# A state space mixer inside an fp32 trunk: two weight units split a layer early, Pool's operations cut, norms in one bank, the last steps in a written order

## The chip, the cores and the metric

One core of a Trainium2 chip runs the whole program. The metric is the device time of one execution in microseconds (us). The engines are TensorE (PE; PEld is its weight load, which overlaps the matmuls), VectorE (DVE), ScalarE (ACT), GpSimd (POOL) and SyncE (SP), which here only issues transfers. Each engine works through its own list of instructions in order, so an instruction that waits holds up all that stands behind it on that engine.

## What is computed

A trunk of two layers on 256 tokens of width 1024, all in float32. Each layer adds half of a SwiGLU network, then a mixer, then half of a second SwiGLU network. The first layer's mixer is the state space one (Mamba-2), which the change touches; the second's is latent attention.

```python
for i in range(2):
    x = x + 0.5 * swiglu(rms_norm(x, ...), ...)
    h = rms_norm(x, norm_w[i, 1])
    x = x + (mamba2_mixer(h, ...) if i == 0 else mla_mixer(h, ...))
    x = x + 0.5 * swiglu(rms_norm(x, ...), ...)

def mamba2_mixer(h, ...):
    proj = h @ w_in                          # z 2048, x 2048, B 1024, C 1024, dt 32
    xbc = silu(causal_depthwise_conv(xbc))   # 4 taps over time
    y = ssd_chunked(xs, softplus(dt + dt_bias), a, bm, cm) + d_skip * xs
    g = y * silu(z)                          # 8 groups of 256 channels
    g = g * rsqrt(mean(g * g over the group) + EPS)
    return (g * norm_w) @ w_out
```

## The kernel before

**Weights.** All weights arrive as one stream of units, mostly of eight 128x128 tiles (512 KB, one transfer on SP's queue). Each unit is split in two reduced parts, a high one by a cast on ACT (`whi`, L131) and the remainder by a subtraction on DVE (`wlo`, L134). A product of a weight tile with an activation is then three matmuls of 256 columns (`mm3`, L227 to L229: high with high, high with low, low with high). There are four raw buffers (AHEAD) and five split ones (SPLIT), so the cast of a unit waits until TensorE has finished with the unit five places ahead of it.

**The mixer.** `ssm` works on eight groups g of 256 channels. It first computes dt, and B and C for the groups 0 and 1, and then runs a loop over g, whose body is written as a list of stages:

- `stage_x` and `stage_z`: two projections each of eight tiles; x goes through `conv` (DVE L421, ACT L431 and L435, one POOL addition of 128x512 in L436, four DVE operations in L439, a Silu on ACT in L443).
- `stage_y(g-1)`: eight small matmuls with the decay matrices `dec` (L609, L612), then on DVE `y` (L619), on POOL the gating `gt` of 128x512 (L624) and the squares of both halves and their sum (`gsq`, L263, L266, L267).
- `stage_a` for two groups on every other turn: decay matrices, by sixteen exponentials on ACT (L569, L572) and masks and products on DVE.
- `stage_bc(g+2)`: B and C of a later group.
- `stage_n(g-1)`: the column sums of the squares on TensorE (L273), then `rsv` on DVE (L277) and a power on POOL that gives `rsc` (L281).
- `stage_t(g)`: x transposed on TensorE (L590), and `xd` on DVE (L595).
- `stage_o(g-2)`, written ahead of `stage_z`: `rsc` spread over the partitions by TensorE (L288), the normalised `gn` on DVE (L639), and its two parts `yh` on ACT (L252) and `yl` on DVE (L253).
- `stage_out(g-3)`: sixteen tiles of the output weights with `yh` and `yl`, 48 matmuls, added up over the groups in the four PSUM banks called acc. The projections use acc banks until the first `stage_out` and after that the four misc banks, as all small results do.

Behind the loop a list of stages finishes the groups 5 to 7. Text names below such as n2 or o7 are `stage_n(2)` or `stage_o(7)`, and y7 likewise.

**Order.** The code's order is only a priority. A scheduler simulates all engines and puts the instructions of each in the order in which they come ready, so that matmuls of several stages interleave.

Of the kernel before, what the change touches and what calls it, by code (L numbers as in the profile page):

```python
# [10 lines left out]
F32 = mybir.dt.float32  # L11
F32R = mybir.dt.float32r
# [7 lines left out]
P = 128  # L20
T = 256
# [44 lines left out]
EARLY = (MLA0 + 6, MLA0 + 11, MLA0 + 12, MLA0 + 17)  # L66


class Stream:
# [15 lines left out]
    def load(self, upto):  # L85
        while self.loaded < min(upto, len(self.sizes)):
            u = self.loaded
            if u in EARLY:
# [17 lines left out]
    def cut(self, upto):  # L106
        while self.split < min(upto, len(self.sizes)):
            u = self.split
            if u in EARLY:
                self.split += 1  # L110
                continue
# [34 lines left out]

    def early(self, pool, u):
# [6 lines left out]
        hi = pool.tile([P, n], F32R, tag=f"hi{u}", name=f"hi{u}", bufs=1)  # L154
        lo = pool.tile([P, n], F32R, tag=f"lo{u}", name=f"lo{u}", bufs=1)
        self.nc.scalar.copy(hi, raw[:, :n])
        self.nc.gpsimd.tensor_tensor(
            out=lo, in0=raw[:, :n], in1=hi.bitcast(F32), op=ALU.subtract
        )
        self.parts[u] = (hi, lo)  # L160
# [25 lines left out]
def trunk(ctx: ExitStack, tc: tile.TileContext, xt, pos, wts, small, consts, out):  # L186
# [81 lines left out]

    def rs_col(acc, n):

        ps = misc_ps()
        for b in range(NB):
# [3 lines left out]
        v = sp.tile([P, NB], F32, tag="rsv", name="rsv")  # L276
        nc.vector.tensor_scalar(  # L277
            out=v, in0=ps[:, :NB], scalar1=1.0 / n, scalar2=EPS, op0=ALU.mult, op1=ALU.add
        )
# [4 lines left out]
    def spread(r):  # L284

        ps = misc_ps()
        for b in range(NB):
# [116 lines left out]

    def ssm(n, nxt):
        with tc.tile_pool(name="mp", bufs=2) as mp:
# [10 lines left out]
            def conv(ps, tiles, dst):  # L417
# [12 lines left out]
                for j, t in enumerate(tiles):  # L430
# [4 lines left out]
                    nc.scalar.activation(b[:, j], up[:, j, 1 : 1 + T], AF.Copy, scale=w(t, 1))  # L435
                nc.gpsimd.tensor_tensor(out=a, in0=a, in1=b, op=ALU.add)  # L436
                for k in (2, 3):
# [103 lines left out]
            def stage_a(g):  # L541
# [10 lines left out]
                nc.scalar.copy(cb, ps[:, : 3 * P])  # L552
                acb = mp.tile([P, 4, T], F32, tag="acb", name="acb")
                nc.sync.dma_start(
# [10 lines left out]
                for hp in range(2):  # L565
                    dec = mp.tile([P, 2, 3 * P], F32, tag="dec", name="dec", bufs=6)
                    for j in range(2):
# [35 lines left out]
            def stage_y(g):  # L603
# [19 lines left out]
                gt = mp.tile([P, 2, T], F32, tag="gt", name="gt")  # L623
                nc.gpsimd.tensor_tensor(out=gt, in0=y, in1=zs, op=ALU.mult)  # L624
                sq = sp.tile([P, T], F32, tag="xsq", name="gsq")
                for j in range(2):
                    add_square(sq, gt[:, j], j == 0)
                st[g, "g"], st[g, "q"] = gt, sq

            def stage_n(g):  # L630
                st[g, "r"] = rs_col(st.pop((g, "q")), 2 * P)

            def stage_o(g):
                gt = st.pop((g, "g"))
                ps = spread(st.pop((g, "r")))
                gn = mp.tile([P, 2, T], F32, tag="tmp", name="gn", bufs=3)
# [41 lines left out]
            def stage_z(g):  # L678
# [7 lines left out]
                st[g, "z"] = zs  # L686

            stage_bc(1)
            last = NG - 1
            for g in range(NG):  # L690
                stage_x(g)
                if g == 0:
                    bias, acd = sums()
                if g > 1:
                    stage_o(g - 2)
                stage_z(g)
# [5 lines left out]
                if g + 2 < NG:  # L702
                    stage_bc(g + 2)
                if g:
                    stage_n(g - 1)
                if g < last:
                    stage_t(g)
                if g > 2:
                    stage_out(g - 3)

            stage_t(last)
            stage_o(last - 1)
            stage_out(last - 2, 0, 4)
# [417 lines left out]
    for i, (f, n) in enumerate(plan):  # L1131
        nxt = n + 1 if i + 1 < len(plan) else None
        if i == 3:
            ep = early.enter_context(tc.tile_pool(name="ep", bufs=1))
# [157 lines left out]
```

## Time and profile before

| | us |
|---|---|
| three runs | 1102.43, 1103.98, 1105.25 |
| median of them | 1103.98 |
| the profiled execution | 1104.49 |
| its span, first to last instruction | 1102.7 |
| TensorE busy in it | 1079.8 |
| the mixer's part of the span | 195.0 to 428.7 |

The profile is of one execution. Its time is 1104.49 us, of which the span covers 1102.7. Busy times overlap between engines. An idle time of TensorE stands in brackets in its row, with the instruction that it waited for. The granted clock stands as a share of full speed: 1.00 is 2.4 GHz and 0.50 is 1.2 GHz.

### The profile page before, as it was taken

The numbers are of one execution on the slowest core, as the hardware profiler recorded it, in microseconds if no ns is written. First come the engines' busy times: TensorE is split into PE (matmuls) and PEld (weight loads), VectorE is DVE, ScalarE is ACT, GpSimd is POOL, SyncE is SP. The second block draws the span as 40 slices with busy tenths as digits, with TensorE's granted clock in tenths as the row PEclk, the third lists the DMA queues.
The fourth block names the chain that finished last, engine by engine and source line by source line (L and its number), as shares of the span: only waits on it lengthen the run. The fifth ranks groups of instructions, "written<-read, shape, count | busy, mean of one in ns | idle before, by whom it ended". The sixth has DMA issues, their size and how long they took to land.

```text
span 1102.7 us, 18308 instructions
## 1 busy us (share of the span) xinstructions
PE 1079.8 (98%) x6886; PEld 964.3 (87%) x6886; DVE 838.8 (76%) x1396; ACT 643.1 (58%) x1105; POOL 195.7 (18%) x201
## 2 busy tenths in 40 slices
PE   8999999999899998999999999999999999999998
PEld 7888888998899998888888988888898688888887
DVE  7877766789978867877777688876779868877663
ACT  6755644667876744666544476664458546655541
POOL 1100013213523235000012101001240544000000
PEclk9999999999999998999999999999999999999999
DMA  8656655565445453655555566655531325656661
GB/s 287 213 189 190 184 188 170 173 197 190 161 163 178 135 185 97 208 187 184 184 191 189 174 210 211 212 196 187 175 105 59 97 87 167 214 186 188 191 200 49
DMA packets 55640, 191.58 MB, mean 174 GB/s; under 512 B 6240, under 2 KB 9088, under 8 KB 55552
## 3 DMA queue, kind: packets, MB, share of 16 engines
q1 hardware_dynamic: 55488, 190.41, 53.0%
q8 instruction: 54, 0.88, 0.3%
q14 instruction: 34, 0.28, 0.1%
q0 software_dynamic: 64, 0.01, 0.0%
HBM read 189.31 MB, written 1.08 MB: 173 GB/s over the span
## 4 chain that ended last, share of the span: by engine, by line
PE 61%; DVE 2%; ACT 0%; issue 0%; ACTq 0%; DVEq 0%
PE acc L238 32%; PE misc L238 17%; PE acc L227 2%; PE acc L228 2%; PE acc L229 2%; PE acc L1072 1%; PE acc L248 1%; PE acc L247 1%; PE acc L249 1%; PE misc L963 1%; PE misc L1032 1%; PE misc L1057 0%; DVE pr L1050 0%; DVE mx L1041 0%; PE misc L1033 0%; PE misc L273 0%
## 5 line engine op out<-in xcount | busy, mean ns | idle before, releaser
L134 DVE TENSOR_TENSOR wlo<-raw,whi 128x1024 fp32r<-128x1024 f32 (+2 forms) x345 | 429.4, 1247 | 155.0 <-ACT whi L131 153.8
L131 ACT CAST whi<-raw 128x1024 fp32r<-128x1024 f32 (+2 forms) x353 | 362.8, 1032 | 252.5 <-PE acc L238 132.9
L238 PE MATMUL misc<-xp,whi 128*128 128x512 f32 x704 | 277.9, 398 | 0.5 <-DVE xp L257 0.5
L238 PE MATMUL acc<-xp,whi 128*128 128x512 f32 x704 | 275.5, 395 | 0.0
L238 PE MATMUL acc<-ap,whi 128*128 128x512 f32 x616 | 215.5, 397 | 0.0
L238 PE MATMUL acc<-xp,wlo 128*128 128x256 f32 x704 | 196.8, 281 | 0.0
L238 PE MATMUL misc<-xp,wlo 128*128 128x256 f32 x704 | 196.4, 281 | 0.3 <-DVE wlo L134 0.2
L238 PE MATMUL acc<-ap,wlo 128*128 128x256 f32 x616 | 167.8, 281 | 0.0
L238 PEld LDWEIGHTS acc<-xp,whi 128*128 128x128 f32 x704 | 131.9, 188 | 32.2
L238 PEld LDWEIGHTS misc<-xp,whi 128*128 128x128 f32 x704 | 131.9, 188 | 24.2 <-DVE xp L257 0.8
L238 PEld LDWEIGHTS misc<-xp,wlo 128*128 128x128 f32 x704 | 132.5, 188 | 8.2 <-DVE wlo L134 0.9
L238 PEld LDWEIGHTS acc<-ap,whi 128*128 128x128 f32 x616 | 113.9, 188 | 25.5
L238 PEld LDWEIGHTS acc<-xp,wlo 128*128 128x128 f32 x704 | 132.8, 189 | 0.7
L238 PEld LDWEIGHTS acc<-ap,wlo 128*128 128x128 f32 x616 | 115.4, 188 | 2.8
L346 ACT COPY g<-misc 128x256 f32<-128x256 f32 x88 | 32.7, 371 | 77.1 <-PE misc L238 77.1
L228 PE MATMUL acc<-xp,whi 128*128 128x256 f32 x264 | 74.6, 283 | 0.0
L227 PE MATMUL acc<-xp,whi 128*128 128x256 f32 x264 | 74.5, 283 | 0.0
L229 PE MATMUL acc<-xp,wlo 128*128 128x256 f32 x264 | 74.2, 281 | 0.0
L263 POOL TENSOR_TENSOR xsq<-x 128x256 f32<-128x256 f32 x5 | 3.1, 612 | 284.8 <-DVE x L402 271.4
L266 POOL TENSOR_TENSOR sq<-x 128x256 f32<-128x256 f32 x35 | 31.7, 912 | 111.2 <-DVE x L402 111.2
L347 DVE TENSOR_TENSOR g<-misc,g 128x256 f32<-128x256 f32 x88 | 37.0, 420 | 18.0 <-ACT g L346 18.0
L227 PEld LDWEIGHTS acc<-xp,whi 128*128 128x128 f32 x264 | 49.7, 189 | 0.3 <-issue 0.3
(260 smaller groups left out, 1889.5 us busy)
## 6 DMA issues: line engine op xcount, KB each, us to landing
raw<-wts SPq DMA_DIRECT2D x341, 512.0 KB, 3.7
acb<-acd SPq DMA_DIRECT2D x8, 512.0 KB, 3.8
raw<-wts SPq DMA_DIRECT2D x8, 256.0 KB, 4.9
raw<-wts SPq DMA_DIRECT2D x4, 384.0 KB, 3.2
x<-xt SPq DMA_DIRECT2D x8, 128.0 KB, 4.5
out<-x SPq DMA_DIRECT2D x8, 128.0 KB, 3.5
raw<-wts SPq DMA_DIRECT2D x4, 192.0 KB, 2.4
sm<-small SPq DMA_DIRECT2D x1, 283.5 KB, 6.4
```

The costliest lines, as they stand in the source:

```text
L131: self.nc.scalar.copy(hi[:, c], raw[:, c])
L134: ins = eng.tensor_tensor(out=lo[:, c], in0=raw[:, c], in1=hi[:, c].bitcast(F32), op=ALU.subtract)
L227: nc.tensor.matmul(o, w[0], h, start=start, stop=False)
L228: nc.tensor.matmul(o, w[0], l, start=False, stop=False)
L229: nc.tensor.matmul(o, w[1], h, start=False, stop=stop)
L238: nc.tensor.matmul(dst, a, b, start=start and i == 0, stop=stop and i == 1)
L247: nc.tensor.matmul(o, h, w[0], start=start, stop=False)
L248: nc.tensor.matmul(o, l, w[0], start=False, stop=False)
L249: nc.tensor.matmul(o, h, w[1], start=False, stop=stop)
L266: nc.gpsimd.tensor_tensor(out=sq, in0=src, in1=src, op=ALU.mult)
L346: nc.scalar.copy(t, ps[:, T:])
L347: nc.vector.tensor_tensor(out=t, in0=ps[:, :T], in1=t, op=ALU.add)
```

## The change

Five edits, all to the mixer but for the first, which reaches into the network ahead of it.

1. The four units of B and C of the groups 0 and 1 (`EARLY_BC`) are loaded and split during the first network, at its steps q = 4, 8, 12 and 16, the high part on ACT and the rest on DVE. They lie in a new pool `sep`, in the buffers that later hold `dec` and `acb`.
2. POOL's operations: the convolution's addition and the gating are each two operations of 128x256 in place of one of 128x512. The squares are one operation on ACT (128x512, L643 of the new code) and one addition on POOL (128x256, L644), in place of three on POOL.
3. `rsv` in `stage_n` is computed by ACT (L288 of the new code) and no more by DVE.
4. `stage_o(g-2)` and `stage_n(g-1)` share one misc bank and stand together behind `stage_bc` (`stage_on`), so that o of a group is now one turn behind its n, at the end of the turn.
5. The stages behind the loop, with the last `stage_out` of the loop, stand in TensorE's list as written (`manual_schedule`): y7 and n6 come sooner, and n and o of the last groups lie between parts of `stage_out`.

```diff
+EARLY_BC = tuple(SSM0 + n for n in range(1, 5))
...
         self.nc.scalar.copy(hi, raw[:, :n])
-        self.nc.gpsimd.tensor_tensor(
+        eng = self.nc.gpsimd if tags is None else self.nc.vector
+        eng.tensor_tensor(
             out=lo, in0=raw[:, :n], in1=hi.bitcast(F32), op=ALU.subtract
         )
...
+        if by_act:
+            nc.scalar.activation(v, ps[:, :NB], AF.Copy, scale=1.0 / n, bias=EPS)
+        else:
+            nc.vector.tensor_scalar(
+                out=v, in0=ps[:, :NB], scalar1=1.0 / n, scalar2=EPS, op0=ALU.mult, op1=ALU.add
+            )
...
-                nc.gpsimd.tensor_tensor(out=a, in0=a, in1=b, op=ALU.add)
+                for j in range(2):
+                    nc.gpsimd.tensor_tensor(out=a[:, j], in0=a[:, j], in1=b[:, j], op=ALU.add)
...
-                acb = mp.tile([P, 4, T], F32, tag="acb", name="acb")
+                acb = sep.tile([P, 4, T], F32, tag="acb", name="acb", bufs=2)
...
-                    dec = mp.tile([P, 2, 3 * P], F32, tag="dec", name="dec", bufs=6)
+                    dec = sep.tile([P, 2, 3 * P], F32, tag="dec", name="dec", bufs=6)
...
-                nc.gpsimd.tensor_tensor(out=gt, in0=y, in1=zs, op=ALU.mult)
-                sq = sp.tile([P, T], F32, tag="xsq", name="gsq")
+                sq = mp.tile([P, 2, T], F32, tag="tmp", name="sq2", bufs=3)
                 for j in range(2):
-                    add_square(sq, gt[:, j], j == 0)
-                st[g, "g"], st[g, "q"] = gt, sq
-
-            def stage_n(g):
-                st[g, "r"] = rs_col(st.pop((g, "q")), 2 * P)
-
-            def stage_o(g):
+                    nc.gpsimd.tensor_tensor(
+                        out=gt[:, j], in0=y[:, j], in1=zs[:, j], op=ALU.mult
+                    )
+                nc.scalar.activation(sq, gt, AF.Square)
+                nc.gpsimd.tensor_tensor(out=sq[:, 0], in0=sq[:, 0], in1=sq[:, 1], op=ALU.add)
+                st[g, "g"], st[g, "q"] = gt, sq[:, 0]
+
+            def stage_n(g, ps=None):
+                st[g, "r"] = rs_col(st.pop((g, "q")), 2 * P, ps, True)
+
+            def stage_o(g, ps=None):
                 gt = st.pop((g, "g"))
-                ps = spread(st.pop((g, "r")))
+                ps = spread(st.pop((g, "r")), ps)
...
+            def stage_on(g):
+
+                ps = misc_ps()
+                if g > 1:
+                    stage_o(g - 2, ps)
+                if g:
+                    stage_n(g - 1, ps[:, T:])
...
-                if g > 1:
-                    stage_o(g - 2)
                 stage_z(g)
...
-                if g:
-                    stage_n(g - 1)
-                if g < last:
-                    stage_t(g)
+                if g == last:
+                    stage_o(last - 2)
+                    break
+                stage_on(g)
+                stage_t(g)
                 if g > 2:
                     stage_out(g - 3)
 
-            stage_t(last)
-            stage_o(last - 1)
-            stage_out(last - 2, 0, 4)
-            stage_y(last)
-            stage_out(last - 2, 4, 8)
-            stage_out(last - 1, 0, 4)
-            stage_n(last)
-            stage_out(last - 1, 4, 6)
-            stage_o(last)
-            stage_out(last - 1, 6, 8)
-            stage_out(last)
+            with tc.manual_schedule(engines={mybir.EngineType.PE}):
+                stage_out(last - 3, 0, 3)
+                stage_t(last)
+                stage_out(last - 3, 3, 8)
+                stage_y(last)
+                stage_n(last - 1)
+                stage_out(last - 2, 0, 4)
+                stage_o(last - 1)
+                stage_out(last - 2, 4, 8)
+                stage_n(last)
+                stage_out(last - 1, 0, 3)
+                stage_o(last)
+                stage_out(last - 1, 3, 8)
+                stage_out(last)
...
+        if i == 0:
+            sep = early.enter_context(tc.tile_pool(name="sep", bufs=1))
+            acb, dec = ("acb", 2), ("dec", 6)
+            homes = [(dec, dec), (dec, dec), (dec, dec), (acb, acb)]
+            ffn(n, nxt, [(sep, u, h) for u, h in zip(EARLY_BC, homes)])
```

Three places show what this does to the engines' lists. The first is DVE's list before, from `y` of group 0 to `rsv` of group 0 (`up` is the scaled input of a convolution, `ca` its sum).

```order
L619 SCALAR_TENSOR_TENSOR y<-xs,sm,misc 128x256 x2
L134 TENSOR_TENSOR wlo<-raw,whi 128x1024
L421 TENSOR_TENSOR up_2047<-acc,rs 128x2x256
L560 TENSOR_TENSOR acb<-acb,cst 128x4x128
L563 TENSOR_TENSOR acm<-acb,cst 128x512
L134 TENSOR_TENSOR wlo<-raw,whi 128x1024 x2
L439 SCALAR_TENSOR_TENSOR ca<-up_2048,sm,ca 128x256 x3
L134 TENSOR_TENSOR wlo<-raw,whi 128x1024
L439 SCALAR_TENSOR_TENSOR ca<-up_2048,sm,ca 128x256
L439 SCALAR_TENSOR_TENSOR ca<-up_2047,sm,ca 128x256 x2
L134 TENSOR_TENSOR wlo<-raw,whi 128x1024
L277 TENSOR_SCALAR rsv<-misc 128x2
```

In the new kernel `rsv` of group 0 stands in ACT's list, which from the squares of group 0 (L643) to it reads so (L133 is the cast to `whi`, L444 and L448 belong to the convolution):

```order
L643 ACTIVATE sq_2712<-gt 128x512
L133 CAST whi<-raw 128x1024
L444 ACTIVATE ca<-up_2060,sm 128x256
L448 ACTIVATE cb<-up_2060,sm 128x256
L444 ACTIVATE ca<-up_2060,sm 128x256
L448 ACTIVATE cb<-up_2060,sm 128x256
L133 CAST whi<-raw 128x1024
L288 ACTIVATE rsv<-misc 128x2
```

So `rsv` left DVE's list, where two convolutions and five splits stood between it and `y`, and both it and the squares now queue between ACT's casts. The second place is POOL's list before, from `rsc` of group 1 to that of group 2.

```order
L281 TENSOR_TENSOR rsc<-rsv,mhalf 128x2
L436 TENSOR_TENSOR ca<-ca,cb 128x512
L624 TENSOR_TENSOR gt<-y,zs 128x512
L263 TENSOR_TENSOR gsq<-gt 128x256
L266 TENSOR_TENSOR sq<-gt 128x256
L267 TENSOR_TENSOR gsq<-gsq,sq 128x256
L281 TENSOR_TENSOR rsc<-rsv,mhalf 128x2
```

The same stretch of POOL's list now, where L640 is the gating, L644 the sum of the squares, L450 the convolution's addition and L294 the power:

```order
L294 TENSOR_TENSOR rsc<-rsv,mhalf 128x2
L640 TENSOR_TENSOR gt<-y,zs 128x256 x2
L644 TENSOR_TENSOR sq_3263<-sq_3263 128x256
L450 TENSOR_TENSOR ca<-ca,cb 128x256 x2
L294 TENSOR_TENSOR rsc<-rsv,mhalf 128x2
```

Between the gating and the column sums POOL now has one operation where it had three, and the one waits for ACT. The third place is TensorE's list at the end of the mixer, before: n7, o7 and the first matmuls of the last `stage_out` (out 7).

```order
L227 MATMUL acc<-yh,whi 128x256
L228 MATMUL acc<-yl,whi 128x256
L229 MATMUL acc<-yh,wlo 128x256
L273 MATMUL misc<-ones,gsq 128x1 x2
L288 MATMUL misc<-cst,rsc 128x128 x2
L227 MATMUL acc<-yh,whi 128x256 x4
```

The same place now (L237 to L239 are the three matmuls of `mm3`, L283 is n7 and L301 o7; eighteen matmuls stand between them, the first and the last three of which are printed):

```order
L283 MATMUL misc<-ones,sq_4648 128x1 x2
L237 MATMUL acc<-yh,whi 128x256
L238 MATMUL acc<-yl,whi 128x256
L239 MATMUL acc<-yh,wlo 128x256
...
L237 MATMUL acc<-yh,whi 128x256
L238 MATMUL acc<-yl,whi 128x256
L239 MATMUL acc<-yh,wlo 128x256
L301 MATMUL misc<-cst,rsc 128x128 x2
```

Before, o7 stood right behind n7 and out 7 right behind o7. Now 18 matmuls stand between n7 and o7, and 30 between o7 and out 7. Counted in the same way in TensorE's lists, the distance from y to n of a group, in matmuls of `mm3`, went from 85 to 93 for group 0, from 75 to 96 for group 2 and from 85 to 76 for group 4; that from n to o of group 0 went from 47 to 53; from o(g-2) to n(g-1), which now share a bank, there are 81, 68, 54, 28 and 69 in the turns 2 to 6.

## Rows read from the trace of the kernel before

**Rows 1.** The page: busy us of each engine, share of the span, instructions.

```profile
PE 1079.8 (98%) x6886; PEld 964.3 (87%) x6886; DVE 838.8 (76%) x1396; ACT 643.1 (58%) x1105; POOL 195.7 (18%) x201
```

**Rows 2.** What TensorE waited for in the mixer: total us, times, longest.

```profile
PE misc L273 <- POOL gsq L267: 4.8, 4, 3.3
PE misc L288 <- POOL rsc L281: 3.2, 2, 2.2
PE acc L227 <- ACT yh L252: 2.1, 2, 1.9
PE acc L228 <- DVE yl L253: 1.1, 1, 1.1
PE misc L609 <- DVE dec L576: 0.2, 1, 0.2
```

**Rows 3.** Stretches: length, busy us of PE, PEld, DVE, ACT, POOL; clock, DMA share, GB/s.

```profile
0.00:195.00 195.00, 192.14 (x1104) 167.86 (x1105) 145.50 (x236) 113.92 (x192) 20.48 (x30) 1.00 0.64 204
255.60:294.50 38.90, 36.54 (x296) 34.59 (x295) 38.49 (x54) 30.81 (x55) 17.52 (x14) 0.96 0.47 157
272.30:275.70 3.40, 3.40 (x16) 2.66 (x12) 3.40 (x7) 3.22 (x7) 0.45 (x1) 0.50 0.68 205
303.00:306.40 3.40, 3.40 (x18) 3.40 (x17) 0.82 (x2) 1.04 (x1) 1.94 (x2) 0.50 0.67 237
419.10:425.90 6.80, 5.79 (x27) 5.79 (x28) 2.61 (x5) 1.53 (x4) 1.42 (x2) 0.50 0.24 80
```

**Rows 4.** TensorE in order of time: start, us, instruction, idle time ahead and its releaser.

```profile
286.99 0.38 PE L288 MATMUL misc<-cst,rsc 128*128 128x128 f32 x2
...
298.18 0.28 PE L228 MATMUL acc<-yl,whi 128*128 128x256 f32 x1
298.30 0.28 PE L229 MATMUL acc<-yh,wlo 128*128 128x256 f32 x1
301.87 0.61 PE L273 MATMUL misc<-ones,gsq 128*128 128x1 f32 x4 [3.28 <-POOL gsq L267]
...
410.82 0.39 PE L228 MATMUL acc<-yl,whi 128*128 128x256 f32 x1 [1.13 <-DVE yl L253]
...
417.73 0.43 PE L288 MATMUL misc<-cst,rsc 128*128 128x128 f32 x2 [1.03 <-POOL rsc L281]
420.11 1.22 PE L227 MATMUL acc<-yh,whi 128*128 128x256 f32 x4 [1.95 <-ACT yh L252]
...
428.50 0.40 PE L238 MATMUL misc<-xp,whi 128*128 128x512 f32 x1
```

**Rows 5.** TensorE at n0 and o0, same columns.

```profile
262.02 0.61 PE L273 MATMUL misc<-ones,gsq 128*128 128x1 f32 x4 [0.21 <-POOL gsq L267]
270.83 0.43 PE L288 MATMUL misc<-cst,rsc 128*128 128x128 f32 x2 [2.15 <-POOL rsc L281]
```

**Rows 6.** DVE in order of time, at rsv of group 0 and gn of group 1.

```profile
269.85 0.15 DVE L277 TENSOR_SCALAR rsv<-misc 128x2 f32<-128x2 f32 x1
...
290.26 0.86 DVE L639 SCALAR_TENSOR_TENSOR gn<-gt,sm,misc 128x256 f32<-128x256 f32 x2
```

**Rows 7.** POOL in order of time, between y 2 and n2.

```profile
294.50 3.96 POOL L624 TENSOR_TENSOR gt<-y,zs 128x512 f32<-128x512 f32 x1 [3.00 <-DVE y L619]
298.54 0.68 POOL L263 TENSOR_TENSOR gsq<-gt 128x256 f32<-128x256 f32 x1
...
300.04 1.77 POOL L267 TENSOR_TENSOR gsq<-gsq,sq 128x256 f32<-128x256 f32 x1
```

**Rows 8.** Groups by shape, in and around the mixer: busy us, mean ns, idle before.

```profile
L131 ACT CAST whi<-raw 128x1024 fp32r<-128x1024 f32 x70 | 72.4, 1046 | 53.5 <-PE acc L228 19.7 <-issue 10.4 <-PE misc L228 9.9
...
L443 ACT ACTIVATE xs<-ca 128x512 f32<-128x512 f32 x8 | 5.0, 630 | 8.3 <-DVE ca L439 8.3
```

**Rows 9.** Of the whole run by shape: the shortest copy on ACT.

```profile
L204 ACT COPY used<-ones 128x1 f32<-128x1 f32 x1 | 0.2, 192 | 0.0
```

**Rows 10.** What ACT waited for in the mixer: total us, times, longest.

```profile
ACT whi L131 <- PE acc L228: 19.7, 9, 4.8
```

More of the change, by code (lines that the diff above doesn't have):

```diff
@@ L87, in load @@
             u = self.loaded
-            if u in EARLY:
+            if u in EARLY + EARLY_BC:
                 self.loaded += 1
@@ L108, in cut @@
             u = self.split
-            if u in EARLY:
+            if u in EARLY + EARLY_BC:
                 self.split += 1
@@ L145, in cut, with early @@
             self.parts[u] = (hi, lo)
-    def early(self, pool, u):
+    def early(self, pool, u, tags=None):
         n = self.sizes[u] * P
@@ L153, in early @@
         )
-        hi = pool.tile([P, n], F32R, tag=f"hi{u}", name=f"hi{u}", bufs=1)
-        lo = pool.tile([P, n], F32R, tag=f"lo{u}", name=f"lo{u}", bufs=1)
+        if tags is None:
+            hi = pool.tile([P, n], F32R, tag=f"hi{u}", name=f"hi{u}", bufs=1)
+            lo = pool.tile([P, n], F32R, tag=f"lo{u}", name=f"lo{u}", bufs=1)
+        else:
+            hi, lo = (
+                pool.tile([P, n], F32R, tag=t, name=f"{w}{u}", bufs=b)
+                for w, (t, b) in zip(("hi", "lo"), tags)
+            )
         self.nc.scalar.copy(hi, raw[:, :n])
-        self.nc.gpsimd.tensor_tensor(
+        eng = self.nc.gpsimd if tags is None else self.nc.vector
+        eng.tensor_tensor(
             out=lo, in0=raw[:, :n], in1=hi.bitcast(F32), op=ALU.subtract
@@ L267, in add_square, with rs_col @@
         nc.gpsimd.tensor_tensor(out=acc, in0=acc, in1=sq, op=ALU.add)
-    def rs_col(acc, n):
-        ps = misc_ps()
+    def rs_col(acc, n, ps=None, by_act=False):
+        ps = misc_ps() if ps is None else ps
         for b in range(NB):
@@ L276, in rs_col @@
         v = sp.tile([P, NB], F32, tag="rsv", name="rsv")
-        nc.vector.tensor_scalar(
-            out=v, in0=ps[:, :NB], scalar1=1.0 / n, scalar2=EPS, op0=ALU.mult, op1=ALU.add
-        )
+        if by_act:
+            nc.scalar.activation(v, ps[:, :NB], AF.Copy, scale=1.0 / n, bias=EPS)
+        else:
+            nc.vector.tensor_scalar(
+                out=v, in0=ps[:, :NB], scalar1=1.0 / n, scalar2=EPS, op0=ALU.mult, op1=ALU.add
+            )
         r = sp.tile([P, NB], F32, tag="rsc", name="rsc", bufs=4)
@@ L282, in rs_col, with spread @@
         return r
-    def spread(r):
-        ps = misc_ps()
+    def spread(r, ps=None):
+        ps = misc_ps() if ps is None else ps
         for b in range(NB):
@@ L403, in ffn, with ssm @@
                 use_x(nxt, d)
-    def ssm(n, nxt):
+    def ssm(n, nxt, sep):
         with tc.tile_pool(name="mp", bufs=2) as mp:
@@ L623, in stage_y @@
                 gt = mp.tile([P, 2, T], F32, tag="gt", name="gt")
-                nc.gpsimd.tensor_tensor(out=gt, in0=y, in1=zs, op=ALU.mult)
-                sq = sp.tile([P, T], F32, tag="xsq", name="gsq")
+                sq = mp.tile([P, 2, T], F32, tag="tmp", name="sq2", bufs=3)
                 for j in range(2):
-                    add_square(sq, gt[:, j], j == 0)
-                st[g, "g"], st[g, "q"] = gt, sq
-            def stage_n(g):
-                st[g, "r"] = rs_col(st.pop((g, "q")), 2 * P)
-            def stage_o(g):
+                    nc.gpsimd.tensor_tensor(
+                        out=gt[:, j], in0=y[:, j], in1=zs[:, j], op=ALU.mult
+                    )
+                nc.scalar.activation(sq, gt, AF.Square)
[4 more added lines that the diff above has]
+            def stage_o(g, ps=None):
                 gt = st.pop((g, "g"))
-                ps = spread(st.pop((g, "r")))
+                ps = spread(st.pop((g, "r")), ps)
                 gn = mp.tile([P, 2, T], F32, tag="tmp", name="gn", bufs=3)
@@ L1132, in trunk @@
         nxt = n + 1 if i + 1 < len(plan) else None
-        if i == 3:
+        if i == 0:
[3 more added lines that the diff above has]
+            ffn(n, nxt, [(sep, u, h) for u, h in zip(EARLY_BC, homes)])
+        elif i == 1:
+            f(n, nxt, sep)
+            early.close()
+        elif i == 3:
             ep = early.enter_context(tc.tile_pool(name="ep", bufs=1))
```

## The prediction

> **What bounds the kernel now.** I read the busy times first [rows 1]: TensorE works 1079.8 of 1102.7 us, no other engine comes near, so the time is TensorE's work plus what it waits, and a stage is worth what it makes TensorE wait or run slow. Next the list of TensorE's waits, cut to the mixer [rows 2]: 11.4 us in five kinds, nearly all on the chain that normalises a group (squares, power, `gn` parts). Then TensorE in order of time, to see where these waits lie [rows 4, 5]. Two large ones are in the loop: 2.15 us ahead of o0, released by the power on POOL, and 3.28 ahead of n2, released by the squares. Behind the loop stand 1.13 (yl6), 1.03 (o7) and 1.95 (yh7), together 4.1. So the loop holds 11.4 - 4.1 = 7.3.
>
> Last the granted clock by stretches [rows 3]. It is 1.00 in the network ahead, but falls to 0.50, the lower of the two levels (1.2 GHz), in three stretches of 3.40, 3.40 and 6.80 us. Each lies shortly behind large idles: 2.15, 3.28, and the pair 1.03 and 1.95. Behind the single 1.13 it did not fall. Two stretches of 3.40 at half speed cost 1.7 each, 3.4 in the loop. For the last I take the rows themselves: out 7 runs from 420.11 to 428.50, 8.39 us for 48 matmuls, which at the pace of two neighbours (298.18 and 298.30, 0.12 apart) need 5.76 [rows 4], so 2.6 is lost.
>
> All that could be won here: loop 7.3 + 3.4 = 10.7, end 4.1 + 2.6 = 6.7, together 17.4. No edit removes matmuls, so 1104.49 - 17.4 = 1087.1 is the floor for the profiled execution.
>
> **Edit 1, the early units.** Four casts and four subtractions move to the first network: at the cast's 1.05 each [rows 8], and the subtraction of the same 128x1024 taken as about as long, some 4 us on ACT and 4 on DVE. There DVE is busy 145.5 and ACT 113.9 of 195 us, and TensorE 192.14 [rows 3], so 40 us or more are free on each. Cost 0 while the ring of split units keeps its lead; if each cast held up the next one and that TensorE, 4 x 1.05 = 4.2. I take 0, since the stretch shows no such hold, and keep 4.2 for the range. On SP four transfers go ahead of later ones, in a stretch whose transfer share is 0.64 [rows 3]: also 0. The gain is at the mixer's head, where TensorE doesn't wait; it is worth something only as room for DVE in the turns 0 to 2, where it is full: 38.49 of 38.90 us [rows 3].
>
> **Edits 2 to 4, the loop.** *o0.* Its 2.15 come from `rsv` 0, which ran on DVE at 269.85 [rows 6], 7.2 us behind the sums that began at 262.02 and ended 0.61 later [rows 5]: it stood behind splits and convolutions, as DVE's list in the section on the change shows. On ACT it stands behind one cast. No row shows a copy of 128x2 on ACT; the nearest is 128x1 at 0.19 [rows 9], and I take 0.2. The chain is then at most 1.05 + 0.2 and a power of 0.7 to 1.8 (the spread of POOL's small operations in [rows 7]), 2 to 3 us, against 53 matmuls x 0.12 = 6.4. The wait goes, and the clock's 1.7 with it. Next late would be `xd` of group 1 on DVE, which ran right behind `rsv`; it keeps DVE's queue.
>
> *n2.* From the gating's begin (294.50) to the end of the squares (300.04 + 1.77 = 301.81) POOL took 7.3 us [rows 7], 3.96 of it the one gating that ran beside busy DVE. Now: two gatings of 128x256 (0.7 to 1.8 each, the two operations of that shape in [rows 7]), a Square of 128x512 on ACT and one addition (0.7 to 1.8). The Square is not in the trace; a Silu of that shape on ACT takes 0.63 [rows 8], and I take that. A sum of 2.7 to 6.0, and 3.5 is likeliest, since a shorter operation next to DVE is also hit less often. That saves 3.8 against a wait of 3.28, and y2 stands 96 matmuls ahead of n2 where it was 75, another 21 x 0.12 = 2.5. The wait goes with 3 us to spare, and its 1.7 of clock. At n4 the distance shrinks by 9 matmuls, 1.1 us, but the chain saves more.
>
> On this the Trainium skill has a figure ("ScalarE: Activation LUTs", section "What ACT_TABLE_LOAD costs"): an operation with immediate scale and bias takes 186 ns and 0.833 ns per element. An estimate from it is 0.61 us for the Square and 0.19 for `rsv`; the sum would be the same.
>
> *New waits.* `rsv` and the Square now stand in ACT's list, o and n in one bank, and o1 follows n1 by only 32 matmuls, 3.8 us, with a convolution's addition ahead of its power on POOL. I expect one such place to be late once: 1.2 us, about the size of the single waits in [rows 4], and 1.7 of clock, 2.9 in all. So the loop gains 10.7 - 2.9 = 7.8, with 10.7 and -4 (the slow rival for one group, below) as ends.
>
> **Edit 5, the end.** *n7* stands 48 matmuls (5.8 us) behind y7; `y` on DVE, two gatings, Square and addition take 0.9 + 1.4 + 0.6 + 0.7 = 3.6 when POOL is beside an idle DVE, up to 5 behind one split. *o7* stands 18 matmuls, 2.2 us, behind n7, whose own 0.5 comes on top; a cast ahead of `rsv` (1.05), 0.2 and 0.7 are 1.95. *out 7* begins 30 matmuls, 3.6 us, behind o7; before, o7 to the end of idle took 420.11 - 417.73 = 2.4 for `yh` [rows 4], and `yl` is one operation later, about 3.0. Each fits, o7 with some 0.7 to spare and yl6 (24 matmuls, 2.9, against 3.0) about level. I leave 0.4. With no idle there is no reason for half clock, so the end gains 6.7 - 0.4 = 6.3. Behind it the next network waits for x of the last `stage_out`: a denser end leaves those additions less cover, 0.3 lost.
>
> **The sum.** 1104.49 - 7.8 - 6.3 + 0.3 = 1090.7. The profiled execution was 0.5 above the median of the runs (1103.98), so 1090.2.
>
> **The rivals.**
> *A. DVE stays the limit of the loop.* For it: 38.49 of 38.90 us in the turns 0 to 2 [rows 3], and the change takes only `rsv` (0.15, [rows 6]) off DVE per group. Then the waits move from POOL's results to `xd`, `y` or `gn`, 2.2 us and 1.7 of clock at two places, 7.8: so of the loop's 7.8 nothing is left, and the end gains its 6.3. 1104.49 - 6.3 + 0.3 - 0.5 = 1098.0. Against it: the squares' chain doesn't need DVE, and y2 has 21 matmuls more.
>
> *B. The shared bank.* The order gives n(g-1) a wait for DVE's read of the bank in o(g-2), although the two use different columns. `gn` of group 1 was done at 291.12 [rows 6], 4.1 us behind its o at 286.99 [rows 4]; the shortest distance is now o3 to n4, 28 matmuls or 3.4 us and the transposes of t5 (0.5 or so). With one more split ahead the read comes 1.5 late: 1.5 + 1.7 of clock = 3.2 at that place, 1093.4; the other distances, 54 and more, are 6.5 us. The rule behind that wait is in the Trainium skill ("PSUM — Partial Sum Buffer", section "PSUM bank collisions raise a hardware error"): two engines must be kept apart by the bank and quadrant, not by the address. No row of the kernel before shows two stages in one bank.
>
> *C. Slower: squares and `rsv` queue behind casts that wait.* ACT's casts wait for TensorE to free a split buffer, 19.7 us in 9 places, 4.8 at most [rows 10]. A Square behind such a cast is 4.8 late, less the 2.7 or so to spare: 2.1 idle and 1.7 clock, 3.8 per group. All eight groups cost 30: 1120.6. It comes out slower than before by over 0.3% (3.3 us, about what a measurement of this kernel tells from no change) from (1107.3 - 1090.2) / 3.8 = 4.5, so five groups. Against it: the order puts only one or two casts ahead of each of them, and TensorE keeps feeding the ring meanwhile.
>
> *D. No gain that counts.* New waits of other kinds eat both parts, at the end too where each step is only 0.7 us from late: 1101 to 1107.
>
> **How the numbers follow.** My forecast, 1086.5 to 1094.5 with B in it: 0.60 (B alone 0.08). A: 0.22. C: 0.07. D: 0.11. Predicted 1090.2. The range must leave out at most 2 in 10: it takes the forecast and A with its spread, 1086.5 to 1099.5, and leaves out C, D and a little of both ends. It holds edit 1's bound (1090.2 + 4.2 = 1094.4). Faster by over 0.3%: the forecast and A, 0.82. Within it: D, 0.11. Slower: C, 0.07.
>
> **What would show it.** In TensorE's waits in the mixer, the entries on the squares and the power gone and the sum under 3 us; no half clock from 400 to the end of the mixer; `rsv` on ACT within 3 us of its sums; the gating's halves near 0.7 to 1.8. Wrong it would be if TensorE waits for `y`, `xd` or `gn` instead (A), if n4 waits for `gn` (B), or if the Squares come behind casts that wait (C). Waits for `wlo` in the first network would show edit 1's cost.

## The result, and the profile after

Four runs of the changed kernel gave 1091.25 to 1092.91 us, median 1091.8, against 1104.62 for the kernel before: a ratio of 0.9887, 95% interval 0.9869 to 0.9906, or 12.5 us less (the ratio is of means; the medians lie 12.8 apart). The forecast was 1090.2. The profiled execution took 1091.99 us, its span 1090.2.

TensorE's waits in the mixer, as in [rows 2], are now (line; what it waited for; total us, times, longest):

```profile
PE acc L239 <- DVE wlo L136: 3.0, 1, 3.0
PE misc L283 <- POOL sq L644: 1.7, 1, 1.7
PE misc L301 <- POOL rsc L294: 0.2, 1, 0.2
PE misc L623 <- DVE dec L590: 0.2, 1, 0.2
PE misc L283 <- DVE gn L656: 0.2, 1, 0.2
```

So 11.4 us became 5.3. The waits of the end (`yh`, `yl`, the power at o7) are gone but for 0.2, and two large single ones are left in the loop. In stretches, as in [rows 3] (length, busy us of PE, PEld, DVE, ACT, POOL; clock, DMA share, GB/s), the mixer, its end and the only stretch at half clock:

```profile
194.20:416.50 222.30, 216.94 (x1812) 210.99 (x1811) 181.38 (x260) 154.45 (x263) 65.10 (x73) 0.99 0.49 164
388.00:416.50 28.50, 28.26 (x242) 27.21 (x239) 19.79 (x30) 15.13 (x22) 9.50 (x12) 1.00 0.46 160
288.50:292.00 3.50, 3.48 (x16) 3.48 (x17) 3.50 (x4) 0.00 (x0) 0.00 (x0) 0.51 0.70 194
```

The mixer went from 233.4 us (195.1 to 428.5) to 222.3, so 11.1 less; of its idle time 6.1 and of half clock 4.3 went. The other 1.4 us of the span lie outside it. 0.85 are ahead of the mixer, and no edit need have made them: the kernel with edit 5 alone, whose first network is that of the kernel before, reaches the mixer at 193.8 in its profile. 0.56 are behind it, where the kernel before had one more stretch of half clock at 859 us, in the attention. The two idles that were left stand in TensorE's list so (start, us, instruction, idle ahead and its releaser):

```profile
261.79 0.61 PE L283 MATMUL misc<-ones,sq 128*128 128x1 f32 x4 [1.73 <-POOL sq L644]
...
288.52 0.58 PE L239 MATMUL acc<-xp,wlo 128*128 128x256 f32 x1 [3.01 <-DVE wlo L136]
```

The first is n0. The second is a projection whose `wlo`, the low part of its weights, came late, and DVE in order of time shows why. It waited 3.51 us for the transfer `acb` of group 4, to do masks (L574, L577) whose exponentials run on ACT from 317 us on, and the splits came behind them:

```profile
272.50 0.88 DVE L656 SCALAR_TENSOR_TENSOR gn<-gt,sm,misc 128x256 f32<-128x256 f32 x2 [0.92 <-PE misc L301]
276.88 0.69 DVE L574 TENSOR_TENSOR acb<-acb,cst 128x512 f32<-128x512 f32 x1 [3.51 <-DMA acb<-acd]
277.49 0.68 DVE L577 TENSOR_TENSOR acm<-acb,cst 128x512 f32<-128x512 f32 x1
...
287.26 2.35 DVE L136 TENSOR_TENSOR wlo<-raw,whi 128x1024 fp32r<-128x1024 f32 x2
```

### The profile page after: what moved, and what is told of

It reads as the page before. It is cut to its first block, busy times and chain, and to the rows that moved or that the text cites. A ratio compares the mean times of both kernels' runs of the same rounds, so it can differ in the third digit from the quotient of the medians.

```text
span 1090.2 us, 18318 instructions
## 1 busy us (share of the span) xinstructions
PE 1072.1 (98%) x6886; PEld 958.8 (88%) x6886; DVE 836.5 (77%) x1388; ACT 648.1 (59%) x1121; POOL 188.7 (17%) x209
## 4 chain that ended last, share of the span: by engine, by line
PE 89%; DVE 6%; ACT 2%; issue 1%; DMA 1%; POOL 0%; SPq 0%; DVEq 0%; POOLq 0%; ACTq 0%
PE acc L248 42%; PE misc L248 22%; PE acc L238 4%; PE acc L237 4%; PE acc L239 4%; PE misc L238 2%; PE misc L237 2%; PE misc L239 2%; DVE wlo L136 1%; DVE ca L453 1%; PE acc L258 1%; PE acc L257 1%; PE acc L259 1%; DVE pr L1077 1%; PE acc L1099 1%
## 5 line engine op out<-in xcount | busy, mean ns | idle before, releaser
L136 DVE TENSOR_TENSOR wlo<-raw,whi 128x1024 fp32r<-128x1024 f32 (+2 forms) x341 | 422.1, 1241 | 144.6 <-ACT whi L133 143.6
L133 ACT CAST whi<-raw 128x1024 fp32r<-128x1024 f32 (+2 forms) x349 | 358.9, 1032 | 235.8 <-PE acc L248 127.8
L248 PE MATMUL acc<-xp,wlo 128*128 128x256 f32 x704 | 196.8, 282 | 0.0
L248 PEld LDWEIGHTS acc<-xp,whi 128*128 128x128 f32 x704 | 131.8, 188 | 32.0
L248 PEld LDWEIGHTS acc<-xp,wlo 128*128 128x128 f32 x704 | 132.7, 188 | 0.8
L239 PE MATMUL acc<-xp,wlo 128*128 128x256 f32 x232 | 66.3, 286 | 3.0 <-DVE wlo L136 3.0
L238 PE MATMUL acc<-xp,whi 128*128 128x256 f32 x232 | 66.2, 286 | 0.0
L237 PE MATMUL acc<-xp,whi 128*128 128x256 f32 x232 | 66.1, 285 | 0.0
L239 PEld LDWEIGHTS acc<-xp,wlo 128*128 128x128 f32 x232 | 44.5, 192 | 3.2 <-DVE wlo L136 3.2
```

The lines of the kernel that those rows point to most:

```text
L133: self.nc.scalar.copy(hi[:, c], raw[:, c])
L136: ins = eng.tensor_tensor(out=lo[:, c], in0=raw[:, c], in1=hi[:, c].bitcast(F32), op=ALU.subtract)
L237: nc.tensor.matmul(o, w[0], h, start=start, stop=False)
L238: nc.tensor.matmul(o, w[0], l, start=False, stop=False)
L239: nc.tensor.matmul(o, w[1], h, start=False, stop=stop)
L248: nc.tensor.matmul(dst, a, b, start=start and i == 0, stop=stop and i == 1)
```

## The experiments

Medians are of 4 to 11 runs; each ratio is against the kernel before, run on the same chip in turns. The ratio is of means, and gains in us below are taken from it; most intervals are some 2 us either way, so differences of 1 to 2 us between two rows are not told from none.

| kernel | median us | ratio, 95% interval |
|---|---|---|
| changed kernel | 1091.8 | 0.9887 (0.9869 to 0.9906) |
| before + edit 5 alone | 1098.88 | 0.9948 (0.9929 to 0.9966) |
| changed, edit 5 undone | 1098.16 | 0.9937 (0.9919 to 0.9956) |
| changed, edit 1 undone | 1094.86 | 0.9917 (0.9902 to 0.9932) |
| changed, squares on POOL | 1090.41 | 0.9877 (0.9862 to 0.9891) |
| changed, gating in one operation | 1093.62 | 0.9901 (0.9881 to 0.9921) |
| changed, rsv on DVE | 1092.66 | 0.9893 (0.9878 to 0.9908) |
| changed, two banks for o and n | 1104.24 | 1.0003 (0.9994 to 1.0012) |
| changed, edit 4 undone | 1106.72 | 1.0023 (1.0013 to 1.0032) |
| changed + late masks | 1087.63 | 0.9850 (0.9830 to 0.9871) |
| the same + sum of group 0 on TensorE | 1088.70 | 0.9859 (0.9842 to 0.9875) |
| late masks + n0 later | 1087.41 | 0.9852 (0.9837 to 0.9868) |
| before + edit 5 + late masks | 1100.75 | 0.9962 (0.9948 to 0.9976) |

### The end alone, and the loop alone

The kernel before with edit 5's list in place of its old end (n6 moved there too):

```diff
+                if g == last:
+                    break
                 if g:
                     stage_n(g - 1)
...
+            with tc.manual_schedule(engines={mybir.EngineType.PE}):
+                stage_out(last - 3, 0, 3)
...
```

> The kernel before with edit 5 alone (the end in a written order for TensorE), all else as before. Theory (loop and end add up, the end is worth what its own idles and half clock were, 4.1 + 2.6 less 0.2 that the changed kernel still shows): 6.5 us below the kernel before, so a ratio near 0.9941, no half clock behind 390 us, the waits of the end (yl, o7, yh) together under 0.6, and the loop's 2.15 and 3.28 still there. Rival (the end needs ACT's rsv and POOL's shorter chain as well): o7 or n7 waits 1 us or more and the clock falls once, gain 3 us or less, ratio 0.997 or more.

It gave 0.9948, 5.7 us, and the interval holds the expected 6.5. The end is as expected, with nothing left of `yl` and `yh`; the loop's waits stand as before:

```profile
PE misc L273 <- POOL gsq L267: 5.4, 4, 3.3
PE misc L288 <- POOL rsc L281: 2.4, 2, 2.2
PE misc L609 <- DVE dec L576: 0.6, 1, 0.6
```

The profiled execution ran 6.83 us at half clock at the wait of n2, where the kernel before had 3.41. The other half, the changed kernel with the old end:

```diff
-                if g == last:
+                if g < last:
+                    stage_on(g)
+                    stage_t(g)
+                else:
                     stage_o(last - 2)
-                    break
-                stage_on(g)
-                stage_t(g)
+                    stage_n(last - 1)
...
-            with tc.manual_schedule(engines={mybir.EngineType.PE}):
...
+            stage_t(last)
+            stage_o(last - 1)
...
```

> The changed kernel with edit 5 undone: edits 1 to 4 and the old end. Theory (loop and end add up): the loop alone is worth 3.9 us in idle and half clock by the two profiles, so a ratio near 0.996, 1100 us, the end idling some 4 us with half clock as before. Rival (edits 2 and 3 shorten the old end's chain too): the end's waits fall to 2 us or less without half clock, ratio 0.992 or less.

0.9937, 7.0 us, between the two. The old end idles 2.0 us here in place of 4.1, with 3.41 us of half clock in place of 6.83, so the edits 1 to 4 help it too; which of them does was not tried.

```profile
PE acc L237 <- ACT yh L262: 1.7, 1, 1.7
PE acc L238 <- DVE yl L263: 0.3, 1, 0.3
```

Alone the halves give 5.7 and 7.0 us, both together 12.5: within their intervals they add up.

### Each of the edits 1 to 3 undone

```diff
-EARLY_BC = tuple(SSM0 + n for n in range(1, 5))
+EARLY_BC = ()
...
-            ffn(n, nxt, [(sep, u, h) for u, h in zip(EARLY_BC, homes)])
+            ffn(n, nxt)
```

> The changed kernel with edit 1 undone: the four units of B and C are split in the mixer again. Theory (edit 1 is worth only room for DVE ahead of y 0, four splits of 1.2 us that lie before TensorE's first wait, so little): TensorE's time from the dt projection to the end of the mixer grows by 0 to 2 us, the total by 0 to 0.2%. Rival (DVE is the limit from the mixer's head on, and every split that comes back is paid): y 0 comes some 5 us later, n0's wait grows from 1.7 to 4 or more with half clock, 4 us or more.

0.9917, some 3 us longer than the changed kernel, so more than the theory and less than the rival (the two intervals overlap a little). TensorE reaches y 0 2.8 us later (248.8 in place of 246.0), and small waits come up for masks' products, `up` and `xs` (0.9, 2.0 and 1.2). Edit 1 is worth about 3 us.

```diff
-                st[g, "r"] = rs_col(st.pop((g, "q")), 2 * P, ps, True)
+                st[g, "r"] = rs_col(st.pop((g, "q")), 2 * P, ps)
```

> The changed kernel with edit 3 undone: rsv on DVE. Theory (rsv on DVE waits behind splits as in the kernel before, 7 us at group 0): a wait ahead of o0 or o1 of 1 to 3 us comes back, with half clock in most cases, +2 to +5 us against the changed kernel. Rival (edit 4, which puts o a turn behind n, is enough by itself): waits ahead of o under 0.5, the time within 1 us of the changed kernel.

0.9893 and no wait over 0.2 ahead of any o: the rival. With o a turn behind n, no cost shows of `rsv` on DVE.

```diff
-                nc.scalar.activation(sq, gt, AF.Square)
+                for j in range(2):
+                    nc.gpsimd.tensor_tensor(out=sq[:, j], in0=gt[:, j], in1=gt[:, j], op=ALU.mult)
```

> The changed kernel with the squares on POOL (two operations of 128x256 in place of ACT's one of 128x512; the halves of gating and convolution and the sum stay). Theory (the Square on ACT takes 1 to 2 us out of the chain from y to n): n0's wait grows from 1.7 to about 3, a wait of 1 us or more comes back ahead of n2 or n4, +2 to +5 us against the changed kernel. Rival (on ACT the Square queues as long as it took on POOL, since POOL waited 18.9 us for it in the eight groups): within 1 us of the changed kernel.

0.9877, no slower than the changed kernel. n0's wait grows to 3.3 as the theory had it, but the wait on `wlo` at 288 falls to 0.2. So no gain of the Square on ACT shows.

```diff
-                for j in range(2):
-                    nc.gpsimd.tensor_tensor(
-                        out=gt[:, j], in0=y[:, j], in1=zs[:, j], op=ALU.mult
-                    )
+                nc.gpsimd.tensor_tensor(out=gt, in0=y, in1=zs, op=ALU.mult)
```

> The changed kernel with the gating as one POOL operation of 128x512 again; the convolution's addition stays in halves. Theory (the 1.73 ahead of n0 arises because a half of a convolution's addition, 1.72 us, came in between the two halves of the gating): that wait falls under 0.5 and no other rises, 1 to 2 us less than the changed kernel, 1090, ratio 0.987. Rival (it is POOL beside a busy DVE that is slow, whatever the sizes): the wait stays at 1 to 3 us, or the gating of 128x512 takes 3 us or more at n2 as it did before, time 1091 to 1095.

0.9901, n0's wait 1.99, and the gating at n2 takes 3.75 us: the rival, though the time is not told from that of the changed kernel. With the gating whole, POOL does both halves of the convolution's addition ahead of it at n0, so nothing comes sooner.

### The shared bank and the place

```diff
             def stage_on(g):
-                ps = misc_ps()
                 if g > 1:
-                    stage_o(g - 2, ps)
+                    stage_o(g - 2)
                 if g:
-                    stage_n(g - 1, ps[:, T:])
+                    stage_n(g - 1)
```

> The changed kernel with o(g-2) and n(g-1) in two misc banks of their own, at the same place at the end of the turn. Theory (the shared bank costs no wait of TensorE for gn; its longest row in the changed kernel is 0.2 us): within 1 us of the changed kernel, its waits ahead of n0 (1.7) and on wlo (3.0) there as before. Rival B (the guard of the shared bank costs waits): 2 us or more less. Third possibility (two banks are short of banks for the projections behind the first stage_out): new waits of projections for a bank, 2 us or more longer.

1.0003: the whole gain is gone, 12.8 us, which none of the three had priced so high. TensorE's waits in the mixer are now these:

```profile
PE misc L283 <- POOL sq L644: 8.3, 3, 3.8
PE acc L239 <- DVE wlo L136: 4.8, 1, 4.8
PE misc L623 <- DVE dec L590: 0.3, 1, 0.3
PE misc L301 <- POOL rsc L294: 0.2, 1, 0.2
```

The end is as good as in the changed kernel (the last row is its one wait). The loop idles longer than in the kernel before and has 13.65 us of half clock, where that had 6.8. No matmul shows a wait for a bank, but the lists differ. Matmuls of `mm3` between y and n of a group, counted in TensorE's lists:

| | g2 | g3 | g4 | g5 |
|---|---|---|---|---|
| before | 75 | 64 | 85 | 48 |
| changed | 96 | 109 | 76 | 76 |
| two banks | 37 | 80 | 63 | 48 |

The two largest waits on the squares, 3.80 and 2.81 us, stand ahead of n2 and n5, where the distance is 37 and 48. Group 5 can be compared row by row, since the same thing happens in both kernels: `gt` is ready, and then ACT, in order, first does the sixteen exponentials of a pair of groups. With two banks, POOL and then ACT's Square:

```profile
378.55 1.43 POOL L640 TENSOR_TENSOR gt<-y,zs 128x256 f32<-128x256 f32 x2 [5.00 <-DVE y L633]
385.97 1.35 POOL L644 TENSOR_TENSOR sq<-sq 128x256 f32<-128x256 f32 x1 [5.99 <-ACT sq L643]
```

```profile
377.68 1.28 ACT L583 ACT_TABLE_LOAD   x1
...
385.27 0.62 ACT L643 ACTIVATE sq<-gt 128x512 f32<-128x512 f32 x1
```

In the changed kernel:

```profile
369.53 1.44 POOL L640 TENSOR_TENSOR gt<-y,zs 128x256 f32<-128x256 f32 x2 [5.00 <-DVE y L633]
376.96 1.36 POOL L644 TENSOR_TENSOR sq<-sq 128x256 f32<-128x256 f32 x1 [5.99 <-ACT sq L643]
```

The chain is as slow in one as in the other, 5.99 us of waiting for the Square included. What differs is that TensorE has 76 matmuls to do meanwhile, and not 48. So at this group the shared bank does not make the chain shorter. It changes where y and n stand in the list.

Why it does so was looked for in lists alone, without a run. The shared bank brings two things: a guard, the dependency that keeps n behind DVE's read of the bank for `gn`, and one bank more for the other stages. A list made with two banks and the guard added by hand (n behind `gn` of the o ahead of it) has n3 and n4 16 and 17 matmuls later, but y2 and n5, where the two large waits are, stay as with two banks. What is left for these is the bank itself, one of four misc banks. That this is the reason was not tried.

Edit 4 undone whole, with o ahead of z again:

```diff
             def stage_on(g):
-                ps = misc_ps()
-                if g > 1:
-                    stage_o(g - 2, ps)
                 if g:
-                    stage_n(g - 1, ps[:, T:])
+                    stage_n(g - 1)
...
+                if g > 1:
+                    stage_o(g - 2)
                 stage_z(g)
```

> The changed kernel with edit 4 undone: o(g-2) again written ahead of z of turn g, one bank each. Theory (with rsv on ACT the wait of o0 is covered by the old distance too, since the chain is 2 to 3 us and the old distance 47 matmuls, 5.6): waits ahead of o under 0.5, within 1.5 us of the changed kernel. Rival (the place of o a turn later is what took the 2.15 away, as rsv back on DVE cost only 0.9): 1 us or more ahead of o0 or o1, mostly with half clock, 2 us or more longer than the changed kernel.

1.0023. TensorE's waits ahead of n and of o in the mixer:

```profile
PE misc L283 <- POOL sq L644: 11.4, 4, 5.8
PE misc L301 <- POOL rsc L294: 0.3, 1, 0.3
```

Ahead of o there is no wait over 0.3, so the theory had the right mechanism for o: with `rsv` on ACT the old place of o does not wait, and with `rsv` on DVE, in the run with edit 3 undone, the new place does not. Either is enough for the 2.15 at o0. But the waits ahead of n are those of two banks and more, 11.4 us in four places (5.8 at n2). The time was on the other side of the chain from where I looked.

### The late masks

One dependency more for both mask operations, on the changed kernel:

```diff
+                for ins in (first, second) if g > 1 else ():
+                    tc.add_manual_dep(
+                        ins.ins, xsilu[-1].ins.name,
...
+                        reason="masks no earlier than x of their turn",
+                    )
```

> The changed kernel with one dependency more: the two mask operations of each pair of decay matrices wait for the Silu of x of their own turn (from the second pair on), so that DVE doesn't do the masks of groups 4 and 5 at 276 us, where it waited 3.5 us for their transfer. Theory (the 3.01 ahead of the late wlo at 285.5 comes from masks done a turn too soon, with the wait for their transfer in DVE's list): that wait falls under 0.5, its 1.7 of half clock goes too, 4.7 us less than the changed kernel, about 1087, ratio 0.9845 against before. Rival (DVE has too much work in the turns 0 to 2 in any order): a wait of 2 us or more of TensorE on wlo, y, xd or gn stays between 245 and 305 us, and the time stays at 1090 or more.

0.9850, 1087.63 us, 4 us below the changed kernel: the theory. The masks of the groups 4 and 5 left the stretch, the wait on `wlo` is gone, and there is no half clock in the mixer (granted clock 1.00 throughout):

```profile
PE misc L283 <- POOL sq L657: 2.8, 2, 2.4
PE misc L301 <- POOL rsc L294: 0.2, 1, 0.2
```

The distances from y to n are shorter again in this list, 76, 89, 76 and 45 for the groups 2 to 5, and n5 does not wait at 45, where two banks had 48 and 2.81 us. What differs there is the chain: the Square stands behind the first of the sixteen exponentials in ACT's list and not behind all, so POOL waits 1.12 us for it in place of 5.99. So the distance covers a long chain, and a short one needs less of it.

```profile
364.92 1.88 POOL L653 TENSOR_TENSOR gt<-y,zs 128x256 f32<-128x256 f32 x2 [5.00 <-DVE y L646]
367.93 1.23 POOL L657 TENSOR_TENSOR sq<-sq 128x256 f32<-128x256 f32 x1 [1.12 <-ACT sq L656]
```

Two tries at the last 2.4, ahead of n0. First, TensorE adds the squares of group 0:

```diff
+            for i, one in enumerate(accs_):
+                nc.tensor.matmul(
+                    ps[:, b : b + 1], one[:, b * P : (b + 1) * P], ones,
+                    start=i == 0, stop=i == len(accs_) - 1,
+                )
...
+                if g:
+                    nc.gpsimd.tensor_tensor(out=sq[:, 0], in0=sq[:, 0], in1=sq[:, 1], op=ALU.add)
```

> The kernel with the late masks (the run before), and in group 0 alone the sum of the two squares is not made by POOL but by TensorE, which adds the column sums of both halves in PSUM, two matmuls of one column more. Theory (the last 2.38 us wait, ahead of n0, is POOL's sum of 0.9 queued behind half a convolution's addition of 1.7): that wait falls under 0.5, 1.5 to 2.4 us less than the kernel with late masks, 1085.5. Rival (the wait moves, to xd, wlo or o0, since DVE is what is late in the turns 0 and 1): a wait of 1.5 us or more of another kind between 245 and 290 us, the time within 1 us of 1087.6.

0.9859, no gain. POOL's sum is out of the chain, and the wait is 1.3 for the Square itself. The mixer idles 1.1 less, but the clock fell behind this shorter wait and cost 1.7. Second, n0 later in the list:

```diff
+                if g == 2:
+                    stage_n(0, None, half[-1])
```

> The kernel with late masks, and TensorE's column sums of group 0 (n0) held behind the first projection of z of turn 2, 23 matmuls or 2.8 us later in its list. Theory (n0 stands in the list where POOL's time beside a busy DVE was taken too short, and nothing needs its result for a turn): the wait of 2.38 ahead of n0 falls under 0.3, no other grows, idle in the mixer under 1.2 us, 1085.3, ratio 0.983. Rival (what is late there is late for the next reader too): y 1 or o0 waits 1 us or more, the time within 1 us of 1087.6.

0.9852. n0 waits no more, and the mixer takes 218.0 us (before this edit 218.2), since four waits of 0.2 to 0.9 take its place (1.1 in two for `xs` ahead of t, and 0.8 in two for `gn` ahead of n1 and n2, these by the guard of the bank). The rival, though no single wait reaches its 1 us. This and the late masks alone are level, the fastest kernels of the study, both faster than the changed kernel by 4 us.

Last, whether the masks were all that was wrong in the loop before: the kernel before with edit 5 and the same dependency.

> The kernel before with edit 5 and the late masks alone (none of the edits 1 to 4). Theory (the loop's waits have several causes: rsv 0 behind splits on DVE, the four POOL operations at n2, masks a turn too soon): the masks free 5.4 us of DVE in the turns 0 to 2, so o0's 2.15 falls under 1, but n2's wait stays at 1 us or more, 1095 us, ratio 0.992. Rival (the masks were the one cause of all that was late in the loop): idle of TensorE in the mixer under 2.5 us, 1090 or less, ratio 0.987 or less.

0.9962, no better than edit 5 alone. o0's wait fell to 0.7, as the theory had it, but 8.6 us of waits for the squares came up, ahead of n1 (5.28), n3 and n5. The distances from y to n did not shrink: 58, 64 and 48 matmuls (57, 64 and 48 in the kernel before). What grew is the gating: in just these groups the masks, now late, run on DVE beside it, and it took 5.20, 3.48 and 3.48 us, where it took 1.69, 1.29 and 1.30 in the kernel before. At n1, POOL and then DVE:

```profile
268.86 5.20 POOL L637 TENSOR_TENSOR gt<-y,zs 128x512 f32<-128x512 f32 x1 [6.14 <-DVE y L632]
```

```profile
268.70 0.68 DVE L563 TENSOR_TENSOR acb<-acb,cst 128x512 f32<-128x512 f32 x1
269.30 0.69 DVE L566 TENSOR_TENSOR acm<-acb,cst 128x512 f32<-128x512 f32 x1
269.90 0.69 DVE L563 TENSOR_TENSOR acb<-acb,cst 128x512 f32<-128x512 f32 x1
270.50 0.69 DVE L566 TENSOR_TENSOR acm<-acb,cst 128x512 f32<-128x512 f32 x1
```

In the changed kernel with late masks the two halves of the gating together took 2.15, 1.88 and 1.88 us in the same groups, the last two beside masks. So the halves, of which no gain showed by themselves, may be what lets the late masks pay; late masks with the gating whole were not run.

## Why the prediction held, and where it didn't

**The end** was priced well: 6.3 forecast, 6.5 in the profile (idle 4.1 to 0.24, half clock 2.6 to none). o7 waits 0.24; the others have their cover.

**The loop** was forecast at 7.8 and gave 3.9 in idle and half clock. 0.2 + 1.7 + 3.0 + 0.2 of idle and 1.7 of clock are left, 6.8 in place of the 2.9 that "New waits" allowed. The failed term is that allowance: I took one wait of 1.2, on o1. There were two, and neither on o1: n0's 1.73, where POOL took 1.73 us for a half of the gating beside DVE's splits and a half of a convolution's addition came in between, and the 3.01 behind masks that came a turn too soon. n0, with 0.21 of wait before, had not been priced at all, and the chain there is hardly shorter: 6.1 us from the gating's begin to the end of the sum, against 6.3. At n2 it took 5.0 (7.3 before; 3.5 was thought likeliest), although the Square took 0.63 and `rsv` 0.16, as priced: the rest is waiting. The loss of 0.3 at the next network, which no row gave, didn't come. Of the signs that were set, no half clock from 400 on, `rsv` within 3 us of its sums (1.6 to 2.8 for the groups 0 to 2) and the halves of the gating (0.73 to 1.73) came true; the sum of waits under 3 did not.

**The match of the total has luck in it.** 6.5 and 3.9 are 10.4, and the mixer gave 11.1. 1.4 more came from outside it: 0.85 ahead of the mixer, as an execution without edit 1 shows too, and 0.56 behind it, where the clock happened to fall in one profile and not in the other.

**The reasons for the loop were wrong in their weights.** I gave o0 to `rsv` on ACT and n2 first to the shorter chain, and the 21 matmuls of distance were a further cover. The runs do not bear these weights out: undone one at a time, `rsv` on ACT, the Square and the halved gating show no cost clear of the noise (0.7, -1.1 and 1.5 us), the early units 3 (I took 0), and the bank 12.8. For o0 that is because either of two edits is enough. I had read the distances in the list, but as given, and did not ask which edit had made them.

**Rival A** (DVE stays the limit) was right on the engine and wrong on the reason: in the turns 0 to 2 the order of DVE's work cost the 3.01 and its clock, as the late masks showed. Its amount counts as well: the four splits that edit 1 took out are worth 3. **Rival B** (the guard costs a wait) had the sign wrong: the guard cost 0.2, and without the shared bank the whole gain was gone. **Rival C** (the Square queues on ACT) is what happens: POOL waited 18.9 us for Squares, 5.99 at g5 behind exponentials rather than casts. The distance in the list covers it there, so TensorE waits only where that is short, as with two banks.

## To carry to other kernels

Where a scheduler sets the order, first count, at each edit by itself, how much work stands between a result and its reader, and only then price the chain: an edit that looks like bookkeeping, here which stages share a bank, can move a stage by more than a shortened operation saves. Then look at what will run beside each link of the chain, since a moved operation can slow the one that it lands on. An engine that works in order is also held up by work that is ready too soon. If it waits for something that nobody needs for a long time, tie that work to its turn.

## What the runs showed of the hardware

The granted clock does not follow from the length of the idle ahead. In the changed kernel and in that with `rsv` on DVE, n0 waits 1.73 us in the same place, and the stretch behind it (the same columns as in the windows above) is at full clock in the first and at half in the second:

```profile
262.50:266.00 3.50, 3.50 (x32) 3.50 (x31) 3.50 (x6) 3.17 (x6) 3.50 (x3) 1.00 0.73 260
```

```profile
262.50:266.00 3.50, 3.50 (x18) 3.50 (x19) 3.50 (x8) 2.38 (x4) 2.94 (x3) 0.51 0.72 228
```

With late masks 2.38 us of idle cost no clock, and with the sum on TensorE 1.32 did. The attention's idles (836 to 861 us in the changed kernel, and much the same in all of them) cost it in the profile of the kernel before and in none of the thirteen others. The prediction read three stretches of half clock in that kernel, behind large idles; this is a fourth, of 3.41 us, behind idles of 0.88 and 1.02 us:

```profile
857.00:864.00 7.00, 5.98 (x31) 4.06 (x31) 6.17 (x15) 2.85 (x8) 5.47 (x8) 0.76 0.22 64
```

Executions of one and the same kernel differ too: of eleven of the kernel with edit 5 and late masks, five took 1097.4 to 1099.1 us at a mean granted clock of 0.997, and six 1100.8 to 1102.6 at 0.994 or 0.995. The profile of that kernel is of one of the six. So 1.7 us per wait is a price that is paid or not, and a difference of that size in one profile proves nothing of the edit.

A gating of 128x256 on POOL took 0.74 us with nothing on DVE beside it (the last row on POOL) and 1.73 beside two of DVE's splits, which took 3.37 in place of the 2.35 above. The other half of that gating, at 259.00, took 0.74, but there DVE's operation beside it took 1.06, where the same took 0.48 at 244.54 with POOL idle. On POOL:

```profile
255.64 1.73 POOL L640 TENSOR_TENSOR gt<-y,zs 128x256 f32<-128x256 f32 x1
...
259.00 0.74 POOL L640 TENSOR_TENSOR gt<-y,zs 128x256 f32<-128x256 f32 x1
...
317.72 0.74 POOL L640 TENSOR_TENSOR gt<-y,zs 128x256 f32<-128x256 f32 x1
```

And on DVE:

```profile
255.07 3.37 DVE L136 TENSOR_TENSOR wlo<-raw,whi 128x1024 fp32r<-128x1024 f32 x2
...
258.97 1.06 DVE L453 SCALAR_TENSOR_TENSOR ca<-up,sm,ca 128x256 f32<-128x256 f32 x1
```

The Trainium skill has the rule for it ("SBUF — State Buffer", section "Who interferes with whom"): a DVE instruction with two SBUF inputs contends with a GpSimd instruction that reads SBUF. The trace agrees. Halving POOL's operations did not avoid it at n0; with late masks the whole gating took up to 5.20 us, and the halves together up to 2.42.
